# Hybrid retention/mLSTM layer on one core: weight sums begun in the first retention heads, mixing PSUM pools swapped, last two gate projections one behind the other

## The chip, the cores and the metric

One core of one Trainium2 chip runs the whole layer as one program. The metric is device time in microseconds (us) of an execution, lower is better. The kernel before takes 1399.98 us, the median of 3 runs between 1396.87 and 1403.07.

## The reference

One decoder layer for 1024 prompt positions and 8 samples of 8 positions, 1088 columns (tokens) together, all in float32:

```python
h = rmsnorm(x, pre_mix_g);  proj = (h @ w_in)          # q, k, v, gate of 4 retention and 4 mLSTM heads, 8 gate rows
ret_y = head_groupnorm(retention_chunked(rotary(q_r), rotary(k_r), v_r, S_ret)) * silu(g_r)
ml_y  = head_groupnorm(mlstm_chunked(q_m, k_m, v_m, i_pre, f_pre, C, n, m)) * sigmoid(o_m)
x = x + rmsnorm(concat([ret_y, ml_y]) @ w_out, post_mix_g)
h2 = rmsnorm(x, pre_ffn_g);  up = h2 @ w_up            # 2 x 2816 columns
conv = causal depthwise convolution of width 3 over up
x = x + rmsnorm((gelu(conv_gate) * conv_val) @ w_down, post_ffn_g)
```

The outputs are x and the new states (retention S, mLSTM C, n, m, the last rows of `up`).

## The kernel before, in words

Activations lie transposed, features on the 128 partitions and tokens along the free axis, in four blocks of 272 columns. Every float32 product is made of three fast ones: both factors are split into a rounded half and the rest (`split_w`, `gain_split`: ACT writes `hi`, DVE subtracts to `lo`), and `dense` (lines 152 to 161) runs 8 x 3 matmuls of 128x272 into one PSUM bank for one weight tile and one block.

**Mixing.** `proj` multiplies one 128-column tile of `w_in` with the four blocks; the weight comes by SyncE (SP) through a staging ring `wst` of two buffers and is split into a ring `whi`/`wlo` of two. The 32 projections go two PSUM banks (`psA`), everything else of the heads six (`psB`). `mix_head` does the four retention heads, then the four mLSTM heads; `front` transposes k and v of a pair of chunks and makes the scores, `pair_of` carries the state, `sample` does the eight samples, `finish` the group norm. Between the pairs of chunks `next(rows)` issues a piece of other work: in retention heads 1 to 3 the chain of the mLSTM gate rows (`gate_rows`, operations on 4x1088 values and two scans on DVE), in the mLSTM heads the weight sums.

**Weight sums.** The up-projection uses Strassen's seven products for 20 of its 22 feature tiles, and these need sums of quarters of `w_up`. `weight_sums` (line 688) makes them on GpSimd (POOL): 40 parts, each of two loads of 256 KB from POOL's own DMA queue, four additions of 128x256 and one store of 512 KB to the scratch tensor `sd`. It uses three buffers, the thirds of the tile `tab`. `tab` also holds the rotation tables (first two thirds) and the retention constants (the last third), so its first two thirds are free once the last retention head has rotated its k (L443) and the last third once that head is finished (L598).

**End of mixing.** The output gates of the mLSTM heads are projections 28 to 31 (`late_gate`: DVE multiplies out of PSUM, L471, ACT takes the sigmoid, L473, DVE multiplies into `yT`, L474). The last two run side by side: for each block both weights, then `mix_split` of that block (ACT `mh` L746, DVE `ml` L747), which makes the operands of `w_out`. Those operands take the memory of `h`. Then `mixctx.close()` gives back the memory of all mixing tiles and the pool `fp` takes the same place; weights 2 and 3 of `w_out` (`wtile`), the accumulators `oacc` and the rows `xr` lie there. `out_proj(0)` runs the eight tiles of `w_out` on block 0, one group of 24 matmuls each.

What sets the order: all instructions are issued in program order by the source, a scheduler at build time sets the order on each engine, and each engine then works through its own list strictly in that order. `tc.issue_after` chains one instruction behind another on the same engine; all weight sums are one chain.

## Time and profile before

| | |
|---|---|
| runs | 1399.98 us median (1396.87 to 1403.07) |
| profiled execution | 1397.98 us, its span 1396.0 us |
| mean granted TensorE clock | 0.989 of full |
| PE busy | 1346.0 us, 96% of the span |
| DVE, ACT, POOL busy | 1025.8, 587.9, 476.9 us |
| weight sums on POOL, first to last | 258.6 to 569.3 us |
| last mixing matmul ends / first `w_out` group is evacuated | 552.8 / 560.0 us |

A busy PE is at its work nearly everywhere; what a change can give back are the stretches where it waits. They are found with the list of waits and then looked at in the order of time. Times within the span are counted from its start.

### The profile page before, as it was taken

The page shows a single profiled execution, that of the slowest core. Times are in us where ns is not written, and L with a number is a line of the kernel's source. Part 1 is how long each engine was busy: PE and PEld are TensorE (multiplying, and loading weights), DVE is VectorE, ACT ScalarE, POOL GpSimd, SP SyncE. Part 2 cuts the span into 40 slices and gives each one's busy share as a digit, 9 for nine tenths or more (in the row PEclk, how much of TensorE's full clock was granted, in tenths as well). Part 3 has the DMA queues.
Part 4 walks back from the last instruction along what each step waited for, and adds up shares of the span by engine and source line. Part 5 has one row for each costly group of instructions (what it writes and reads, how often), then busy time and mean ns, then how long its engine had stood idle before and what let it go on. Part 6 is the DMA issues. An engine that isn't in the chain of part 4 may idle for free.

```text
span 1396.0 us, 26912 instructions
## 1 busy us (share of the span) xinstructions
PE 1346.0 (96%) x10545; PEld 1320.9 (95%) x10545; DVE 1025.8 (73%) x2023; ACT 587.9 (42%) x1102; POOL 476.9 (34%) x605
## 2 busy tenths in 40 slices
PE   7999899999999998699999999999999999999995
PEld 7899899999999998699999999999999999999995
DVE  7845985465475578457889987787787788996677
ACT  6423642312222334345565443443343355554563
POOL 4200000129669769200443322212222216782000
PEclk9999999999999999799999999999999999999998
DMA  6111112227876986523314444334444359533363
GB/s 238 61 46 64 48 63 62 93 81 215 206 167 228 211 178 193 202 80 97 111 60 139 162 141 139 125 122 140 147 139 138 110 166 320 181 118 97 91 215 128
DMA packets 92878, 192.80 MB, mean 138 GB/s; under 512 B 16208, under 2 KB 41040, under 8 KB 92240
## 3 DMA queue, kind: packets, MB, share of 16 engines
q1 hardware_dynamic: 80592, 149.14, 32.8%
q0 software_dynamic: 12160, 41.95, 11.7%
q8 instruction: 83, 1.36, 0.4%
q14 instruction: 43, 0.35, 0.1%
HBM read 134.58 MB, written 56.47 MB: 137 GB/s over the span
## 4 chain that ended last, share of the span: by engine, by line
PE 68%; POOL 12%; DVE 8%; DMA 6%; issue 5%; ACT 2%; DVEq 0%; SPq 0%; ACTq 0%; POOLq 0%
POOL tab L700 10%; PE up_S L972 6%; PE up_S L971 6%; PE up_S L970 6%; PE dn L1167 5%; PE dn L1169 5%; PE dn L1168 5%; PE up_A L971 4%; PE up_A L970 4%; PE up_A L972 4%; PE in L161 4%; PE in L159 4%; PE in L160 4%; DMA tab<-in_wu 2%; DMA sd<-tab 2%
## 5 line engine op out<-in xcount | busy, mean ns | idle before, releaser
L159 PE MATMUL in<-hh,wh_in 128*128 128x272 f32 x1024 | 303.0, 296 | 10.9 <-ACT hh L199 6.4
L161 PE MATMUL in<-hh,wl_in 128*128 128x272 f32 x1024 | 300.5, 294 | 1.0 <-DVE wl_in L147 0.9
L160 PE MATMUL in<-hl,wh_in 128*128 128x272 f32 x1024 | 299.4, 293 | 1.2 <-DVE hl L200 1.2
L159 PEld LDWEIGHTS in<-hh,wh_in 128*128 128x128 f32 x1024 | 194.8, 190 | 13.7 <-ACT hh L199 6.4
L160 PEld LDWEIGHTS in<-hl,wh_in 128*128 128x128 f32 x1024 | 194.8, 190 | 3.7 <-issue 2.1
L161 PEld LDWEIGHTS in<-hh,wl_in 128*128 128x128 f32 x1024 | 194.3, 190 | 2.5 <-DVE wl_in L147 1.5
L145 ACT ACTIVATE wh_up<-st_up 128x1024 fp32r<-128x1024 f32 x84 | 80.5, 959 | 165.2 <-PE up_S L971 99.5
L700 POOL TENSOR_TENSOR tab<-tab 128x256 f32<-128x256 f32 x160 | 131.9, 835 | 20.2 <-DMA tab<-in_wu 12.9
L147 DVE TENSOR_TENSOR wl_up<-st_up,wh_up 128x1024 fp32r<-128x1024 f32 x84 | 95.5, 1137 | 8.4 <-ACT wh_up L145 8.4
L944 DVE TENSOR_TENSOR Uv<-Uv,up_S 128x272 f32<-128x272 f32 (+1 forms) x200 | 66.6, 375 | 46.3 <-PE up_S L972 46.3
L1096 DVE TENSOR_TENSOR rb<-rb 128x544 fp32r<-128x544 f32 x78 | 74.0, 955 | 35.3 <-ACT rb L1095 35.2
L1000 POOL TENSOR_TENSOR act<-act 128x544 f32<-128x544 f32 x44 | 70.6, 1604 | 78.3 <-DMA bd<-act 53.3
L700 POOL DMA_DIRECT2D tab<-in_wu x80 | 56.8, 717 | 89.0 <-DVE k_r L443 32.4
L1116 POOL TENSOR_TENSOR wd<-wd 128x512 f32<-128x512 f32 x44 | 74.4, 1718 | 25.1 <-issue 11.2
L1095 ACT ACTIVATE rb<-rb 128x544 fp32r<-128x544 f32 x78 | 50.6, 651 | 75.1 <-DMA rb<-bd 69.6
L985 DVE SCALAR_TENSOR_TENSOR c<-Uv,vec,c 128x1024 f32<-128x1024 f32 (+1 forms) x88 | 70.0, 798 | 8.9 <-ACT c L983 8.9
L985 DVE SCALAR_TENSOR_TENSOR c<-Ug,vec,c 128x1024 f32<-128x1024 f32 x88 | 67.5, 806 | 1.4 <-ACT c L983 1.4
L983 ACT ACTIVATE c<-Ug,vec 128x1024 f32<-128x1024 f32 (+1 forms) x44 | 34.7, 835 | 52.6 <-DVE Ug L948 46.9
L623 POOL TENSOR_TENSOR vx_r<-vts,cst 64x1024 f32<-64x1024 f32 x3 | 5.9, 1963 | 143.1 <-ACT vts L537 143.1
L145 ACT ACTIVATE wh_in<-st_in 128x1024 fp32r<-128x1024 f32 x32 | 33.9, 1058 | 48.9 <-PE in L160 45.9
L159 PE MATMUL out<-mh,wh_out 128*128 128x272 f32 x128 | 39.7, 310 | 13.5 <-ACT wh_out L145 11.1
L147 DVE TENSOR_TENSOR wl_in<-st_in,wh_in 128x1024 fp32r<-128x1024 f32 x32 | 40.7, 1272 | 10.6 <-ACT wh_in L145 9.8
(541 smaller groups left out, 4648.6 us busy)
## 6 DMA issues: line engine op xcount, KB each, us to landing
rb<-bd SPq DMA_DIRECT2D x76, 272.0 KB, 2.8
tab<-in_wu POOLq DMA_DIRECT2D x80, 256.0 KB, 4.8
sd<-tab POOLq DMA_DIRECT2D x40, 512.0 KB, 4.2
st_up<-sd SPq DMA_DIRECT2D x40, 512.0 KB, 3.9
bd<-act SPq DMA_DIRECT2D x33, 544.0 KB, 4.6
st_in<-in_wi SPq DMA_DIRECT2D x32, 512.0 KB, 4.4
st_up<-in_wu SPq DMA_DIRECT2D x24, 512.0 KB, 3.4
wd<-in_wd SPq DMA_DIRECT2D x44, 256.0 KB, 5.0
```

The costliest lines, as they stand in the source:

```text
L145: nc.scalar.activation(hi, x, AF.Copy)
L147: eng.tensor_tensor(lo, x, hi.bitcast(F32), ALU.subtract)
L159: nc.tensor.matmul(ps, hi[:, ws], xh, start=k == 0, stop=False)
L160: nc.tensor.matmul(ps, hi[:, ws], xl, start=False, stop=False)
L161: nc.tensor.matmul(ps, lo[:, ws], xh, start=False, stop=k == KT - 1)
L700: last["sums"] = f(*args)
L970: nc.tensor.matmul(ps, wh[:, c], xh[:, k, n], start=k == 0, stop=False)
L971: nc.tensor.matmul(ps, wh[:, c], xl[:, k, n], start=False, stop=False)
L972: nc.tensor.matmul(ps, wl[:, c], xh[:, k, n], start=False, stop=k == 3)
L985: nc.vector.scalar_tensor_tensor(c, u(i), cw(i), c, ALU.mult, ALU.add)
L1096: nc.vector.tensor_tensor(lo, x, hi.bitcast(F32), ALU.subtract)
L1116: nc.gpsimd.tensor_tensor(quad(p, out), quad(p, x), quad(p, y), op)
```

## The change

1. **Weight sums earlier and with a buffer of their own.** A new tile `wq` (128x1024) takes the place of the rings `wt` and `qs` of the mLSTM heads, in the long-lived pool `mp` just behind `tab`. The first 13 parts use `wq` alone, load, add, store, one after the other with nothing fetched ahead; they are issued in the retention heads 0 to 2, from the early gates of head 0 on. Parts 13 to 17, issued in retention head 3, use the first two thirds of `tab` and `wq` with two fetched ahead; parts 18 to 39, issued in the mLSTM heads, use the three thirds of `tab` as before. The chain now begins behind the last square of `square_sum`.
2. **POOL work moved to DVE.** The three memsets of the gate rows and the multiplication `vx` of retention heads 0 to 2 go to DVE.
3. **PSUM pools swapped**: `psB` (six banks) first, then `psA` (two), so that the first banks of the pool that follows are those of `psB`.
4. **Projections 30 and 31** run one behind the other; `mix_split` follows each block of 31.

```diff
     mixctx = ExitStack()
+    psB = mixctx.enter_context(tc.tile_pool(name="psB", bufs=6, space=PSUM))
     psA = mixctx.enter_context(tc.tile_pool(name="psA", bufs=2, space=PSUM))
-    psB = mixctx.enter_context(tc.tile_pool(name="psB", bufs=6, space=PSUM))
...
+    wq = mp.tile([P, 2, 2, 2 * P], F32, name="wq")
...
-        nc.gpsimd.memset(rst, 1.0)
+        nc.vector.memset(rst, 1.0)
...
                 for i in range(NH):
                     proj((12 + i, early_gate(i)))
+                    next(wsums)
...
-                wt = m2.tile([P, 2, P], F32, tag="wt", name=f"wt_{nmc}")
+                wt, qs = (wq[:, turns["wq"] % 2, i].rearrange("p (i n) -> p i n", i=2) for i in range(2))
...
-            e = nc.vector if hid > 2 else nc.gpsimd
-            e.tensor_tensor(vx, vt[:TS, 0, :W].unsqueeze(1).broadcast_to([TS, NB, W]),
+            nc.vector.tensor_tensor(vx, vt[:TS, 0, :W].unsqueeze(1).broadcast_to([TS, NB, W]),
...
             next(rows, None)
+            if hid > 2 or i % 2 == 0:
+                next(wsums, None)
...
+        own = wq.rearrange("p a b n -> p (a b) n")
+        free = [tab[:, i * D:(i + 1) * D].rearrange("p (b n) -> p b n", b=4) for i in range(3)]
...
+        def stretch(i0, i1, tiles, ahead):
+
+            for i in range(i0, min(i0 + ahead, i1)):
+                fetch(i, tiles[(i - i0) % len(tiles)])
+            for i in range(i0, i1):
                 j, c = parts[i]
...
+                g = tiles[(i - i0) % len(tiles)]
+                if ahead == 0:
+                    fetch(i, g)
+                a11, a22, a12, a21 = (g[:, n, :] for n in range(4))
+                for o_, x, y, op in ((a21, a11, a21, ALU.subtract), (a22, a22, a21, ALU.subtract),
+                                     (a11, a22, a11, ALU.add), (a12, a12, a22, ALU.subtract)):
+                    queued(nc.gpsimd.tensor_tensor, o_, x, y, op)
+                queued(nc.gpsimd.dma_start, sd[j][:, :, cols(c)], g)
+                if 0 < ahead and i + ahead < i1:
+                    fetch(i + ahead, tiles[(i + ahead - i0) % len(tiles)])
                 yield

+        yield from stretch(0, 13, [own], 0)
+        yield from stretch(13, 18, [free[0], free[1], own], 2)
+        yield from stretch(18, len(parts), free, 2)
...
-    proj((30, late_gate(6)), (31, late_gate(7)), done=mix_split)
+    proj((30, late_gate(6)))
+    proj((31, late_gate(7)), done=mix_split)
```

How the built programs differ at three places. On POOL, behind the last square (`sq1`), the kernel before has the `vx` of three heads and the memsets, and then the weight sums in `tab`:

```order
L206 TENSOR_TENSOR sq1_130<-x3_93 128x272
L623 TENSOR_TENSOR vx_r0_1405<-vts2_268,cst_81 64x8x128
L357 MEMSET yT2_803 4x1088
L359 MEMSET yT2_803 4x8
L360 MEMSET yT2_803 4x8
L623 TENSOR_TENSOR vx_r1_2017<-vts1_267,cst_81 64x8x128
L623 TENSOR_TENSOR vx_r2_2638<-vts0_266,cst_81 64x8x128
L700 DMA tab_82<-in_wu 128x2x256 x4
L700 TENSOR_TENSOR tab_82<-tab_82 128x256 x4
L700 DMA sd_276<-tab_82 512x1x256
```

Now the sums follow the last square at once, thirteen times load, add, store in `wq`:

```order
L206 TENSOR_TENSOR sq1_131<-x3_94 128x272
L705 DMA wq_83<-in_wu 128x2x256 x2
L705 TENSOR_TENSOR wq_83<-wq_83 128x256 x4
L705 DMA sd_277<-wq_83 512x1x256
L705 DMA wq_83<-in_wu 128x2x256 x2
```

Nothing on POOL waits for the heads any more until the first part that uses `tab`.

On DVE in retention head 1, among the gate rows (`yT2`, `yT3`, `fg` are their rows; `k_r1` is the rotated k, `in5_0` block 0 of its projection), before, two scans (L362, L368) and eight short ones (L372) stand ahead of the addition that completes block 0 of k (L445):

```order
L354 SCALAR_TENSOR_TENSOR fg_1543<-fg_1543,yT2_803 4x1088
L443 TENSOR_TENSOR k_r1_1640<-in5_0_1777,tab_82 128x272
L444 TENSOR_TENSOR sw_kr10_1802<-sw_kr10_1802,tab_82 128x272
L445 TENSOR_TENSOR q_r1_1639<-q_r1_1639,sw_qr13_1765 128x272
L362 SCALAR_TENSOR_TENSOR yT2_803<-yT2_803,fg_1543 4x1088
L368 SCALAR_TENSOR_TENSOR yT3_804<-fg_1543,yT3_804 4x1024
L372 SCALAR_TENSOR_TENSOR yT3_804<-fg_1543,small_275,yT3_804 4x8 x8
L445 TENSOR_TENSOR k_r1_1640<-k_r1_1640,sw_kr10_1802 128x272
```

Now only the large memset stands between, and the scans come behind it, the one that needs the memsets (L363) later still:

```order
L444 TENSOR_TENSOR k_r1_1690<-in5_0_1827,tab_82 128x272
L445 TENSOR_TENSOR sw_kr10_1852<-sw_kr10_1852,tab_82 128x272
L355 SCALAR_TENSOR_TENSOR fg_1593<-fg_1593,yT2_804 4x1088
L358 MEMSET yT2_804 4x1088
L616 COPY qx_271<-q_r1_1689 128x8x8
L446 TENSOR_TENSOR k_r1_1690<-k_r1_1690,sw_kr10_1852 128x272
L444 TENSOR_TENSOR k_r1_1690<-in5_1_1858,tab_82 128x272
L445 TENSOR_TENSOR sw_kr11_1883<-sw_kr11_1883,tab_82 128x272
L369 SCALAR_TENSOR_TENSOR yT3_805<-fg_1593,yT3_805 4x1024
L373 SCALAR_TENSOR_TENSOR yT3_805<-fg_1593,small_276,yT3_805 4x8 x8
```

The two scans have moved from ahead of block 0 of k to behind it.

On DVE at the end of mixing (`z_7` and `in31_3` are the last gate and its block 3; `ml_10`, `ml_11` the operands of blocks 2 and 3, `wl_out1` the second weight of `w_out`), before:

```order
L471 TENSOR_TENSOR z_7_6540<-in31_3_6778,rb_83 128x272
L747 TENSOR_TENSOR ml_10_6742<-yT0_801,mh_10_6741 128x2x272
L747 TENSOR_TENSOR ml_10_6742<-yT1_802,mh_10_6741 128x2x272
L147 TENSOR_TENSOR wl_out1_6845<-st_out1_6842,wh_out1_6844 128x1024
L747 TENSOR_TENSOR ml_11_6744<-yT2_803,mh_11_6743 128x2x272
L747 TENSOR_TENSOR ml_11_6744<-yT3_804,mh_11_6743 128x2x272
```

Now, with `ml_01` the second half of blocks 0 and 1:

```order
L472 TENSOR_TENSOR z_7_6619<-in31_3_6742,rb_84 128x272
L758 TENSOR_TENSOR ml_10_6731<-yT0_802,mh_10_6730 128x2x272
L758 TENSOR_TENSOR ml_10_6731<-yT1_803,mh_10_6730 128x2x272
L475 TENSOR_TENSOR yT3_805<-yT3_805,z_7_6619 128x272
L758 TENSOR_TENSOR ml_01_6657<-yT3_805,mh_01_6656 128x2x272
L147 TENSOR_TENSOR wl_out1_6806<-st_out1_6803,wh_out1_6805 128x1024
```

Between the last evacuation and `wl_out1` stand two more operations of the gates and splits.

## Rows read from the trace of the kernel before

**Rows 1.** The page, part 1: busy time, share and count of each engine.

```profile
PE 1346.0 (96%) x10545; PEld 1320.9 (95%) x10545; DVE 1025.8 (73%) x2023; ACT 587.9 (42%) x1102; POOL 476.9 (34%) x605
```

**Rows 2.** The list of waits of PE over the whole span: what waited, for what, us in total, times, longest.

```profile
PE out L159 <- ACT wh_out L145: 11.1, 2, 10.7
...
PE x_r L525 <- DVE k_r L445: 2.9, 1, 2.9
...
PE in L159 <- DVE A_m L598: 1.5, 1, 1.5
...
PE in L159 <- DVE z L471: 0.9, 1, 0.9
...
PE in L159 <- DVE q_r L443: 0.8, 2, 0.7
```

**Rows 3.** PE in order of time at the end of mixing: start, duration, operation, and in brackets the idle time before it and what ended it.

```profile
552.51 0.29 PE L161 MATMUL in<-hh,wl_in 128*128 128x272 f32 x1
...
555.22 0.36 PE L159 MATMUL out<-mh,wh_out 128*128 128x272 f32 x1 [2.42 <-ACT mh L746]
...
573.74 0.56 PE L159 MATMUL out<-mh,wh_out 128*128 128x272 f32 x1 [10.72 <-ACT wh_out L145]
```

**Rows 4.** PE by stretches: length, busy time (matmuls), granted clock, DMA share, GB/s.

```profile
556.00:559.40 3.40, 3.40 (x17) 0.51 0.47 176
...
573.70:580.00 6.30, 5.86 (x24) 0.50 0.97 360
```

**Rows 5.** ACT in order of time in the first block of the output projection: `oacc` and `mo` evacuate a group, `wh_out` and `woh` split a weight.

```profile
572.30 0.40 ACT L807 ACTIVATE oacc<-out 128x272 f32<-128x272 f32 x1 [8.59 <-DMA sd<-tab]
...
573.82 1.06 ACT L145 ACTIVATE wh_out<-st_out 128x1024 fp32r<-128x1024 f32 x1
...
582.60 1.06 ACT L145 ACTIVATE woh<-st_out 128x1024 fp32r<-128x1024 f32 x1
...
589.62 1.05 ACT L145 ACTIVATE woh<-st_out 128x1024 fp32r<-128x1024 f32 x1
...
593.48 0.49 ACT L805 ACTIVATE mo<-out,vec 128x272 f32<-128x272 f32 x1 [2.14 <-PE out L161]
...
596.52 0.49 ACT L805 ACTIVATE mo<-out,vec 128x272 f32<-128x272 f32 x1 [2.26 <-PE out L161]
```

**Rows 6.** POOL in order of time: the last square, the first load whose buffer is the last third of `tab`, the last store.

```profile
48.34 0.77 POOL L206 TENSOR_TENSOR sq<-x 128x272 f32<-128x272 f32 x1 [0.38 <-DVE sums_sb L210]
...
306.43 0.72 POOL L700 DMA_DIRECT2D tab<-in_wu  x1 [12.46 <-DVE A_r L598]
...
568.55 0.74 POOL L700 DMA_DIRECT2D sd<-tab  x1 [0.30 <-POOL tab L700]
```

**Rows 7.** The additions of the weight sums by their line (ns minimum/median/maximum, first and last start), and from the page's DMA issues the loads and stores of the sums and the loads of `w_out` (KB each, median us to landing).

```profile
L700 POOL TENSOR_TENSOR tab<-tab x160: 714/738/1797, 267.7 to 567.5; 128x256 f32<-128x256 f32 x160
...
tab<-in_wu POOLq DMA_DIRECT2D x80, 256.0 KB, 4.8
sd<-tab POOLq DMA_DIRECT2D x40, 512.0 KB, 4.2
...
st_out<-in_wo SPq DMA_DIRECT2D x8, 512.0 KB, 4.7
```

**Rows 8.** DVE in order of time in retention head 1, among the gate rows.

```profile
158.76 2.41 DVE L362 TENSOR_TENSOR_SCAN yT<-yT,fg 4x1088 f32<-4x1088 f32 x1
161.09 2.25 DVE L368 TENSOR_TENSOR_SCAN yT<-fg,yT 4x1024 f32<-4x1024 f32 x1
163.27 1.16 DVE L372 TENSOR_TENSOR_SCAN yT<-fg,small,yT 4x8 f32<-4x8 f32 x8
164.36 0.42 DVE L445 TENSOR_TENSOR k_r<-k_r,sw_kr 128x272 f32<-128x272 f32 x1
...
173.69 0.28 DVE L666 COPY S_r<-u_r 128x128 f32<-128x128 f32 x1
```

**Rows 9.** DVE beside an idle and a busy POOL. The split of `w_in` weights from 60 to 250 us and from 306 to 526 us (busy us, mean ns | idle before); two operations of 128x544 by line (ns minimum/median/maximum); and all engines by stretches (length; busy us of PE, PEld, DVE, ACT, POOL; clock, DMA share, GB/s).

```profile
L147 DVE TENSOR_TENSOR wl_in<-st_in,wh_in 128x1024 fp32r<-128x1024 f32 x11 | 13.4, 1220 | 2.3 <-ACT wh_in L145 2.3
...
L147 DVE TENSOR_TENSOR wl_in<-st_in,wh_in 128x1024 fp32r<-128x1024 f32 x12 | 15.7, 1306 | 2.9 <-ACT wh_in L145 2.1
...
L747 DVE TENSOR_TENSOR ml<-yT,mh x16: 712/1246/1265, 538.8 to 563.4; 128x544 fp32r<-128x544 f32 x16
...
L835 DVE TENSOR_TENSOR xr<-xr x8: 710/718/726, 608.4 to 698.6; 128x544 f32<-128x544 f32 x8
...
40.00:60.00 20.00, 18.51 (x144) 17.98 (x143) 18.73 (x41) 10.28 (x23) 6.52 (x8) 1.00 0.19 64
...
125.00:150.00 25.00, 25.00 (x190) 23.05 (x190) 19.83 (x68) 14.23 (x31) 0.00 (x0) 1.00 0.30 92
150.00:175.00 25.00, 21.11 (x167) 20.40 (x166) 24.94 (x52) 12.76 (x24) 1.15 (x3) 1.00 0.08 24
...
306.00:450.00 144.00, 144.00 (x1134) 137.33 (x1133) 83.11 (x252) 38.09 (x110) 114.86 (x151) 1.00 0.75 198
525.00:550.00 25.00, 22.57 (x178) 22.16 (x177) 20.39 (x35) 9.77 (x19) 23.10 (x29) 1.00 0.60 188
```

**Rows 10.** The multiplication `vx` on DVE as the mLSTM heads have it, and a one-input DVE operation on 4x1088 values, by line.

```profile
L623 DVE TENSOR_TENSOR vx_m<-vts,cst x4: 1226/1254/1408, 331.2 to 491.8; 64x1032 f32<-64x1032 f32 x4
...
L342 DVE TENSOR_SCALAR yT<-yT x1: 708/708/708, 145.7 to 145.7; 4x1088 f32<-4x1088 f32 x1
```

More of the change, by code (lines that the diff above doesn't have):

```diff
@@ L205, in square_sum @@
             if k:
-                nc.gpsimd.tensor_tensor(o_, x[:, k, :], x[:, k, :], ALU.mult)
+                last["sums"] = nc.gpsimd.tensor_tensor(o_, x[:, k, :], x[:, k, :], ALU.mult)
             else:
@@ L356, in gate_rows @@
         rst = e
-        nc.gpsimd.memset(rst, 1.0)
+        nc.vector.memset(rst, 1.0)
         rp, rs_ = chunked(rst)
-        nc.gpsimd.memset(rp[:, :, 0:1], 0.0)
-        nc.gpsimd.memset(rs_[:, :, 0:1], 0.0)
+        nc.vector.memset(rp[:, :, 0:1], 0.0)
+        nc.vector.memset(rs_[:, :, 0:1], 0.0)
         bb = w1
@@ L477, in hybrid_layer_kernel @@
     EARLY = (0, 1, 2, 3)
+    turns = {"wq": 0}
     early = []
@@ L545, in front @@
                     nc.tensor.matmul(flat2(0), sel[:, 0, hd, :], uihl[:, cs_], start=True, stop=False)
-                wt = m2.tile([P, 2, P], F32, tag="wt", name=f"wt_{nmc}")
+                wt, qs = (wq[:, turns["wq"] % 2, i].rearrange("p (i n) -> p i n", i=2) for i in range(2))
+                turns["wq"] += 1
                 for i, c in enumerate(cs):
@@ L556, in front @@
                                           flat2(1).rearrange("p (s l) -> p s l", s=NB)[:, :, LS - 1])
-                qs = m2.tile([P, 2, P], F32, tag="qs", name=f"qs_{nmc}")
                 qv = q[:, c0 * CH:c0 * CH + L * n].rearrange("p (i n) -> p i n", i=L)
@@ L621, in sample @@
             vx = m2.tile([TS, NB, 129], F32, tag="vx", bufs=1, name=f"vx_{nm}")[:, :, :W]
-            e = nc.vector if hid > 2 else nc.gpsimd
-            e.tensor_tensor(vx, vt[:TS, 0, :W].unsqueeze(1).broadcast_to([TS, NB, W]),
-                            cst[:TS, C_BLK:C_BLK + NB].unsqueeze(2).broadcast_to([TS, NB, W]), ALU.mult)
+            nc.vector.tensor_tensor(vx, vt[:TS, 0, :W].unsqueeze(1).broadcast_to([TS, NB, W]),
+                                    cst[:TS, C_BLK:C_BLK + NB].unsqueeze(2).broadcast_to([TS, NB, W]), ALU.mult)
             if ml:
-                e.tensor_tensor(sb, sb, dec[:, 8:16].unsqueeze(2).broadcast_to([P, NB, W]), ALU.mult)
+                nc.vector.tensor_tensor(sb, sb, dec[:, 8:16].unsqueeze(2).broadcast_to([P, NB, W]), ALU.mult)
             step = 3 if ml else 4
@@ L694, in weight_sums @@
         cols = lambda c: slice(c * 256, c * 256 + 256)
-        held = []
+        own = wq.rearrange("p a b n -> p (a b) n")
+        free = [tab[:, i * D:(i + 1) * D].rearrange("p (b n) -> p b n", b=4) for i in range(3)]
         def queued(f, *args):
-            with tc.issue_after(last["sums"].ins) if "sums" in last else nullcontext():
+            with tc.issue_after(last["sums"].ins):
                 last["sums"] = f(*args)
-        def fetch(i):
-            if i < len(parts):
-                j, c = parts[i]
-                g = tab[:, i % 3 * D:(i % 3 + 1) * D].rearrange("p (b n) -> p b n", b=4)
-                for q in range(2):
-                    queued(nc.gpsimd.dma_start, g[:, q::2, :], a["wu"][j, q].rearrange("p (b n) -> p b n", b=2)[:, :, cols(c)])
-                held.append(g)
@@ L710, in weight_sums, with fetch @@
-        fetch(0)
-        fetch(1)
-        for i, (j, c) in enumerate(parts):
-            g = held.pop(0)
-            a11, a22, a12, a21 = (g[:, i, :] for i in range(4))
-            for o_, x, y, op in ((a21, a11, a21, ALU.subtract), (a22, a22, a21, ALU.subtract),
-                                 (a11, a22, a11, ALU.add), (a12, a12, a22, ALU.subtract)):
-                queued(nc.gpsimd.tensor_tensor, o_, x, y, op)
-            queued(nc.gpsimd.dma_start, sd[j][:, :, cols(c)], g)
-            fetch(i + 2)
-            if c:
+        def fetch(i, g):
+            j, c = parts[i]
+            for q in range(2):
+                queued(nc.gpsimd.dma_start, g[:, q::2, :], a["wu"][j, q].rearrange("p (b n) -> p b n", b=2)[:, :, cols(c)])
@@ L721, in weight_sums @@
                 yield
+        yield from stretch(0, 13, [own], 0)
+        yield from stretch(13, 18, [free[0], free[1], own], 2)
+        yield from stretch(18, len(parts), free, 2)
+    wsums = weight_sums()
     rows = iter(())
@@ L730, in hybrid_layer_kernel @@
         pass
-    rows = weight_sums()
     for hd in range(NH):
         mix_head(hd, True)
-    for _ in rows:
+    for _ in wsums:
         pass
```

## The prediction

> **What bounds the kernel now.** I read the page's busy times first: PE is busy 96% of the span [rows 1], so no other engine is the bound, and a change can only give back time in which PE waits or runs at a lower clock. The list of waits says where: of its long entries one stands far ahead, 11.1 us in which the output projection waited for the split weight `wh_out`; then come 2.9 us for a rotated k, 1.5 for `A_m`, 0.9 for a gate evacuation and 0.8 for the rotation of q [rows 2]. In the order of time the end of mixing shows it. The last mixing matmul ends at 552.8, the first group of the output projection begins 2.42 us late, and 10.72 us are lost before the third [rows 3]. ACT tells why: it stood 8.59 us in front of the evacuation `oacc` until the last store of the weight sums had landed, and the splits of weights 2 and 3 stand behind that [rows 5]. `oacc` and these weights lie where `tab` lay, and POOL issued its last store only at 568.55 [rows 6]. The clock adds to it: granted 0.51 from 556 to 559.4 and 0.50 from 573.7 to 580 [rows 4], that is the lower of its two levels (1.2 of 2.4 GHz), each time after PE had waited. The eighth group's evacuation follows its matmuls at 596.5 [rows 5], so from the last mixing matmul to the end of block 0 are 43.6 us. A group without waits takes 3.04 us (596.52 less 593.48 [rows 5]), eight take 24.3: 19.3 us are lost here.
>
> **Part 1, the weight sums.** Do they now end in time? One part in `wq` alone: the second load is issued 0.7 after the first and lands 4.8 later, four additions of 0.74, 4.2 until the store has landed [rows 7], 0.3 in front of it [rows 6]: about 13 us. Thirteen parts from the last square at 49 [rows 6] take until about 219. Two thirds of `tab` come free with head 3's k; the first addition in them started at 267.7 [rows 7]. The last third comes free at 306.4 [rows 6], and parts 13 to 18 fit between. Before, the 39 parts from then until ACT went on at 572.3 took 265.9 us, 6.8 each, with every stall in them. Now 21 are left: 306 + 21 x 6.8 = 449. So `tab` is free some 100 us before it is wanted, and the stall of 10.72 us goes for certain; it would come back only if a part took over 11.7 us ((552.8 - 306.4) / 21).
>
> What is late next? Call E the end of the last mixing matmul. Weight 0 of `w_out` takes the ring place of projection 30, free 12 us before E, so group 0 can begin at E; its operands (`mh_00`, `ml_00` to `ml_01`) need the end of block 1 of projection 31, 6 us before E, and about 3.5 us of DVE at 0.71 a piece without POOL beside it [rows 9]. Weight 1 takes the place of projection 31, free only at E. Its ACT split waits behind five `mh` pieces and a sigmoid, its DVE split behind `ml_10` and `ml_01`: ready near E + 4.3, while group 0 ends at E + 3.0. Wait 1.1. Weight 3 uses the staging buffer of weight 1: load from E + 4.3, landing 4.7 later [rows 7], ACT split 1.06: E + 10. On PE the first matmuls of group 3 stand ahead of most of group 2, so group 2 waits for it too: from E + 7.3 to E + 10, 2.7 us. Weights 4 to 7 then have a cycle of load and two splits near 7.3 us for two buffers, against 6.1 of PE: I count 1.4 us of waits together. A fall of the clock as between 556 and 559.4 costs 3.4 - 17 x 0.127 = 1.3 us [rows 4], and it came after 2.42 and 0.89 us of waits; after a single wait of 2.9 in the stretch from 150 to 175 it did not come (clock 1.00 [rows 9]). I take half, 0.7. Sum: 24.3 + 1.1 + 2.7 + 1.4 + 0.7 = 30.2 instead of 43.6, **13.4 us gained**. The bounds: 19.3 if nothing waits; if weights 2 to 7 come at the pace at which they came before, a pair in 7.0 to 8.8 us (573.82, 582.60, 589.62 [rows 5]), say 3.9 each, block 0 ends at E + 10 + 23.4 + 1.3 = 34.7 and 8.9 are gained.
>
> **Part 2, POOL work on DVE, and POOL's new company.** The order on DVE changes with it. The memset of 4x1088 costs DVE 0.7 (as the one-input operation of that size [rows 10]). With it the scheduler has put both scans behind block 0 of k. Before, that k waited for 2.41 + 2.25 + 1.16 us of scans [rows 8] and PE for it 2.9 [rows 2]. Now k is ready about 4.5 us earlier, and PE does not wait there. But it comes then to the state copy `S_r`, before at 173.69 [rows 8], which stands behind the same operations: I put it at 172.2, so 1.5 us of the 2.9 remain gained. The wait of 0.7 us for q [rows 2] in the same chain goes too, since the large gate operation now stands behind that q. `vx` costs DVE 1.25 [rows 10] three times, in places where PE has matmuls; in head 1 the POOL `vx` had held DVE up as long. Gain 2.2.
>
> Against this stands POOL's arithmetic, which now runs while heads 0 and 1 need DVE: 3 us of every 13, 23%. The nearest rows: with POOL busy 114.86 of 144 us the split `wl_in` took 1306 ns instead of 1220, 7% more; with POOL busy 23.1 of 25 us `ml` took 1075 ns as a mean (16.5 us for 16), a like operation beside an idle POOL 718, half as much again [rows 9]. Scaled to 23% that is 2 to 13%. DVE is full from 150 to 175 (24.94 of 25 [rows 9]) and PE waits for it there; with the stretches from 40 to 60 and 125 to 150 (18.73 and 19.83 [rows 9]) 63 us of DVE are exposed: 1.3 to 8.2 us. Most of these operations read two SBUF tensors, but PE has slack in half of these stretches; I take 2.5, nearer the lower row, which holds more operations. Net of part 2: **0.3 lost**, between 3.6 gained (all waits of the heads gone, no contention) and 8.2 lost.
>
> The Trainium skill, "SBUF — State Buffer", section "SBUF: two separate sides", says that DVE and GpSimd share one port pair under an exclusive lock, held for the whole instruction, and that the loser blocks fully, also where the DVE operation has two SBUF inputs. The `ml` rows [rows 9] look like it, the `wl_in` rows far less; taken to the letter in every one of the additions it is the second rival below.
>
> **Parts 3 and 4.** Side by side, projections 30 and 31 held both banks of `psA`; PE waited 0.9 us for an evacuation [rows 2]. One behind the other this goes: 0.9. `A_m` cost 1.5 [rows 2]; PE now comes there 1.2 us earlier, but DVE has some six operations in front of `A_m` that POOL no longer slows by up to 0.36 each, as it did `ml` [rows 9], 2 us: 0.7 gained, between 1.2 lost and 1.5 gained. The swapped pools give groups 0 and 1 banks that are long free; the wait of 2.42 us is counted in part 1.
>
> **Sum.** Against the profiled execution, 1397.98 us: -13.4 + 0.3 - 0.9 - 0.7 = -14.7, so 1383.3. The median of the runs is 2.0 above the profiled one: **1385 us** for the median. What this measurement can tell from no change is about 0.5%, 7 us.
>
> **Rivals.** *Weights bound block 0* (12%). The stall goes, but block 0 runs at the pace of its weights, gain 8.9 as above: -8.9 + 0.3 - 1.6 = -10.2, 1390. For it: the SP queue has 1.7 MB of other loads (two of 544 KB, one of 396, one of 256) in front of weight 4. Against: these are issued at E + 6 now and have landed when weight 4 is needed.
>
> *POOL holds DVE up in the retention heads* (12%, 5% of it slower). One mechanism at one place: 52 additions of 0.74 us [rows 7], 38.5 us, beside the DVE chains of heads 0 to 2, on which PE hangs. If each addition held DVE up in full and PE with it, 38.5 would stand in the sum in place of 2.5, which is then 21.3 slower: 1421. It decides from the point where 17.2 of the 38.5 us reach PE, 45%; between 10 and 24 us it is no measurable change, about 1400. Against: in the mLSTM heads POOL was busy 80% of the time and PE did not wait at all (144.00 of 144 [rows 9]). For it: DVE is not full there, and in head 0 it is.
>
> *The stall stays* (4%). If the parts with one buffer take so long that the rest still ends after E, only the 1.6 us of parts 3 and 4 remain, some 1399. Part 1 shows how far away that is.
>
> **How the numbers follow.** The forecast has 72%, its own range 1380 to 1391: from 19.3 at the boundary to some 9. The first rival lies in 1387 to 1394. Faster by over 0.5% (under 1393) are the forecast and most of the first rival: 81%. Within 0.5%: the mild form of the second, the third and a little of the others, 13%. Slower: 6%. The range for 8 in 10 goes from 1378 to 1396: the lower end is the boundary without any wait and the retention waits half gone, the upper one contention near its upper bound (8.2 instead of 2.5) together with weights at the old pace.
>
> **What would show it.** Right: the last store on POOL before 470 us; no wait of ACT or PE for a store `sd`; between E and the end of block 0 about 30 us with two waits of PE, 1 and near 3 us, for `wl_out` and `wh_out`; PE's wait for k in head 1 under 1 us. Wrong: PE idle that rises by over 5 us before 260; a part in `wq` of over 16 us; a new wait before E for an operand `mh` or `ml`, since `mix_split` now begins later; or block 0 over 35 us.

## The result and the profile after

The changed kernel takes 1385.44 us, the median of 6 runs between 1384.45 and 1387.14; the kernel before, on the same chip, 1398.86 (6 runs, 1393.23 to 1403.07). The ratio is 0.9908, 95% interval 0.9885 to 0.9930: 13.4 us less. In a later set of runs it was 0.9873 (0.9858 to 0.9888). The profiled execution took 1387.14 us (span 1385.4), the longest of its six; this matters below.

The list of waits of PE after, to be read against [rows 2]: what waited, for what, us in total, times, longest. The 11.1 us for `wh_out` are 0.4, and the waits for `mh`, for `A_m` and for `z` ahead of the last projections are gone. New or longer are 1.8 for q, 1.3 for `rcol` (a small product in retention head 0), 1.2 for `S_r` (0.3 before), 1.1 for `wol` (0.7 before), 1.1 for `z`, and 0.9 each for `woh` and for an output matmul whose releaser the view does not name ("issue").

```profile
PE in L159 <- DVE q_r L444: 1.8, 1, 1.8
...
PE o_r L664 <- DVE S_r L668: 1.2, 1, 1.2
PE out L161 <- DVE wol L147: 1.1, 2, 0.7
...
PE x_r L528 <- DVE k_r L446: 0.7, 1, 0.7
PE out L159 <- ACT wh_out L145: 0.4, 1, 0.4
```

PE in order of time at the end of mixing (start, duration, operation, idle time before it), as [rows 3]. The last row is the sum of squares over the third block of the output projection, a fixed place that serves below as the end of this stretch.

```profile
554.06 0.29 PE L161 MATMUL in<-hh,wl_in 128*128 128x272 f32 x1
555.43 0.36 PE L159 MATMUL out<-mh,wh_out 128*128 128x272 f32 x1 [1.08 <-DVE z L472]
...
562.64 0.36 PE L159 MATMUL out<-mh,wh_out 128*128 128x272 f32 x1 [0.89 <-issue]
...
563.54 0.40 PE L159 MATMUL out<-mh,wh_out 128*128 128x272 f32 x1 [0.41 <-ACT wh_out L145]
...
570.60 0.39 PE L159 MATMUL out<-mh,woh 128*128 128x272 f32 x1 [0.88 <-ACT woh L145]
...
571.86 0.39 PE L161 MATMUL out<-mh,wol 128*128 128x272 f32 x1 [0.75 <-DVE wol L147]
...
578.51 0.39 PE L161 MATMUL out<-mh,wol 128*128 128x272 f32 x1 [0.37 <-DVE wol L147]
...
638.04 0.73 PE L186 MATMUL ssqb_po<-oacc,ones 128*128 128x272 f32 x2 [0.44 <-DVE oacc L821]
```

The same sum in the kernel before:

```profile
649.95 0.73 PE L186 MATMUL ssqb_po<-oacc,ones 128*128 128x272 f32 x2 [0.44 <-DVE oacc L809]
```

So from the end E of the last mixing matmul, 554.35 (554.06 + 0.29), to that sum are 83.69 us; before they were 649.95 - 552.80 = 97.15. The boundary gave 13.46. But E itself is 1.55 later than before (1.17 if both are counted from PE's first matmul). And 1.3 us are lost again behind that sum: from 670.1 to 673.5 PE had half the clock, behind a wait of 2.52 us for the sum over the fourth block; in the kernel before the same wait, 2.53 us, was not followed by a lower clock.

POOL after: the first part, the last store from `wq`, the first load into `tab`, the last store of all ([rows 6] has its place before, 568.55).

```profile
49.52 1.62 POOL L705 DMA_DIRECT2D wq<-in_wu  x2
53.88 4.36 POOL L705 TENSOR_TENSOR wq<-wq 128x256 f32<-128x256 f32 x4 [2.74 <-DMA wq<-in_wu]
...
221.63 0.75 POOL L705 DMA_DIRECT2D sd<-wq  x1 [0.30 <-POOL wq L705]
260.26 0.71 POOL L705 DMA_DIRECT2D tab<-in_wu  x1 [37.88 <-DVE k_r L444]
...
446.82 0.74 POOL L705 DMA_DIRECT2D sd<-tab  x1 [0.30 <-POOL tab L705]
```

ACT in the first block, as [rows 5]: the splits of weights 2 and 3 and of 4, and the eighth group. No wait for `sd` is left.

```profile
561.49 2.00 ACT L145 ACTIVATE wh_out<-st_out 128x1024 fp32r<-128x1024 f32 x2
...
569.48 1.06 ACT L145 ACTIVATE woh<-st_out 128x1024 fp32r<-128x1024 f32 x1 [1.74 <-DMA st_out<-in_wo]
...
585.10 0.49 ACT L817 ACTIVATE mo<-out,vec 128x272 f32<-128x272 f32 x1 [2.74 <-PE out L161]
```

By stretches, as [rows 4] (length; busy time of PE, PEld, DVE, ACT, POOL; clock, DMA share, GB/s): PE keeps the full clock over the whole boundary, where it had fallen to half twice.

```profile
553.00:584.00 31.00, 26.63 (x200) 25.30 (x200) 17.84 (x26) 18.78 (x33) 0.46 (x4) 1.00 0.53 176
```

### The profile page after: what moved, and what is told of

It is laid out like the page before. It is cut to its first block, busy times and chain, and to the rows that moved or that the text cites. A ratio compares the mean times of both kernels' runs of the same rounds, so it can differ in the third digit from the quotient of the medians.

```text
span 1385.4 us, 26923 instructions
## 1 busy us (share of the span) xinstructions
PE 1346.3 (97%) x10545; PEld 1319.4 (95%) x10545; DVE 1019.1 (74%) x2029; ACT 588.4 (42%) x1102; POOL 477.8 (34%) x599
## 3 DMA queue, kind: packets, MB, share of 16 engines
q8 instruction: 83, 1.36, 0.4%
## 4 chain that ended last, share of the span: by engine, by line
PE 86%; DVE 8%; ACT 2%; issue 2%; DMA 2%; DVEq 0%; SPq 0%; ACTq 0%
PE in L161 9%; PE in L160 8%; PE in L159 8%; PE up_S L984 6%; PE up_S L983 6%; PE up_S L982 6%; PE dn L1179 4%; PE dn L1181 4%; PE dn L1180 4%; PE up_A L983 4%; PE up_A L982 4%; PE up_A L984 4%; PE out L161 2%; PE out L160 2%; PE out L159 2%
## 5 line engine op out<-in xcount | busy, mean ns | idle before, releaser
L705 POOL TENSOR_TENSOR tab<-tab 128x256 f32<-128x256 f32 x104 | 82.4, 802 | 11.0 <-DMA tab<-in_wu 6.6
L705 POOL TENSOR_TENSOR wq<-wq 128x256 f32<-128x256 f32 x56 | 55.1, 994 | 48.9 <-DMA wq<-in_wu 46.6
L705 POOL DMA_DIRECT2D tab<-in_wu x52 | 36.8, 713 | 61.3 <-DVE k_r L444 41.9
```

What stands on the lines that cost most here:

```text
L705: last["sums"] = f(*args)
```

## The experiments

Two places of every profile are compared in this table: E counted from the start of PE's first matmul (that start varies by 0.8 us between executions), and the stretch from E to the sum over the third block. The chips differ: on them the kernel before had medians from 1398.86 to 1403.99, so the ratio to the kernel before on the same chip stands beside each time. The changed kernel itself was timed in two sets (rows after and e11); e1 to e4 and e12 ran on one chip, e5 to e8 on a second, e9 to e11 on a third. Where medians of different chips are compared below, part of the difference can be the chip's.

| run | E | E to sum | median us (runs) | ratio (95%) |
|---|---|---|---|---|
| before | 546.43 | 97.15 | 1398.86 (6) | |
| after | 547.60 | 83.69 | 1385.44 (6) | 0.9908 (0.9885-0.9930) |
| e1 part 2 alone | 546.13 | 97.45 | 1399.31 (12) | 0.9970 (0.9952-0.9988) |
| e2 parts 3, 4 alone | 545.29 | 103.29 | 1402.26 (12) | 0.9988 (0.9972-1.0004) |
| e3 parts 1, 2 | 546.99 | 83.70 | 1385.49 (5) | 0.9866 (0.9844-0.9887) |
| e4 13 parts without additions | 544.74 | 83.89 | 1384.84 (4) | 0.9862 (0.9840-0.9884) |
| e5 sums from head 2 | 544.91 | 84.81 | 1385.54 (6) | 0.9907 (0.9891-0.9923) |
| e6 part 2 undone | 557.80 | 84.80 | 1398.33 (12) | 1.0000 (0.9986-1.0015) |
| e7 weights 2, 3 elsewhere | 545.33 | 86.97 | 1389.45 (6) | 0.9930 (0.9911-0.9946) |
| e8 = e5 + e7 | 545.92 | 86.15 | 1387.17 (6) | 0.9922 (0.9905-0.9940) |
| e9 weights 4, 5 elsewhere | 545.31 | 80.95 | 1382.29 (4) | 0.9853 (0.9839-0.9866) |
| e10 vx on POOL | 556.54 | 84.89 | 1398.20 (5) | 0.9965 (0.9951-0.9978) |
| e11 after again | 544.70 | 84.42 | 1384.46 (4) | 0.9873 (0.9858-0.9888) |
| e12 = e5 + e9 | 545.18 | 80.99 | 1380.86 (5) | 0.9841 (0.9827-0.9854) |

**Which part makes the gain (e1 to e3).** e1 is the kernel before with part 2 alone:

```diff
-        nc.gpsimd.memset(rst, 1.0)
+        nc.vector.memset(rst, 1.0)
...
-            e = nc.vector if hid > 2 else nc.gpsimd
+            e = nc.vector
```

> The kernel before, with only the memsets and the vx products of the retention heads moved from POOL to DVE; the weight sums still begin in the mLSTM heads. If the new order on DVE in head 1 is a gain by itself and the additions of POOL are what made the last mixing matmul late in the changed kernel (theory): PE's wait for the rotated k falls from 2.9 to under 1.5 us, its wait for q goes, the last mixing matmul ends near 551 instead of 552.8, the stall for the weight sums stays near 11 us, and the run takes about 2 us less, 1396 to 1397. If DVE's extra work itself made it late (rival): the last mixing matmul ends at 554 or later and the run is 1 to 3 us slower than the kernel before.

The wait for k fell to 1.68 us and the stall stayed at 10.79, but E came only 0.3 us earlier, not 2: the wait for q stayed, and 2.2 us of waits stood ahead of E for gate evacuations. The median is 4.7 us below that of the kernel before, which spread there from 1397.5 to 1410.3; the profile shows no gain at the boundary, so where those 4.7 are from stays open. DVE's added work did not make the mixing late.

e2 is the kernel before with parts 3 and 4 alone:

```diff
+    psB = mixctx.enter_context(tc.tile_pool(name="psB", bufs=6, space=PSUM))
     psA = mixctx.enter_context(tc.tile_pool(name="psA", bufs=2, space=PSUM))
-    psB = mixctx.enter_context(tc.tile_pool(name="psB", bufs=6, space=PSUM))
...
-    proj((30, late_gate(6)), (31, late_gate(7)), done=mix_split)
+    proj((30, late_gate(6)))
+    proj((31, late_gate(7)), done=mix_split)
```

> The kernel before, with only the swapped PSUM pools and projections 30 and 31 one behind the other. Theory (the early weight sums make the gain): ACT still waits for the last store of the sums, near 568.5, PE still stalls by 10 us or more, since the 1.6 us won ahead of it are waited away in front of the same store; 1397 to 1399, 0 to 1.6 us gained. Rival (the banks and the projections make most of the gain): the stall shrinks to under 3 us and the run takes 1386 to 1389.

The waits of 1.5 and 0.9 us ahead of E went and E came 1.1 earlier, but then ACT stood 12.98 us in front of the store and PE 14.95. In order of time, PE and ACT of e2:

```profile
555.18 0.57 PE L159 MATMUL out<-mh,wh_out 128*128 128x272 f32 x1 [3.86 <-ACT mh L746]
...
579.02 0.57 PE L159 MATMUL out<-mh,wh_out 128*128 128x272 f32 x1 [14.95 <-ACT wh_out L145]
```

```profile
577.58 0.40 ACT L808 ACTIVATE oacc<-out 128x272 f32<-128x272 f32 x1 [12.98 <-DMA sd<-tab]
```

What was won ahead of the store was waited away in front of it. The last store itself was issued at 573.84, 5.3 us later than in the kernel before, so the stretch from E on is longer by more than the 1.1 us that were won (6.1); what made it later this run does not show. The time is no different from the kernel before. e3 is the changed kernel with both these edits undone (pools in the old order too):

```diff
...
-    proj((30, late_gate(6)))
-    proj((31, late_gate(7)), done=mix_split)
+    proj((30, late_gate(6)), (31, late_gate(7)), done=mix_split)
```

> The changed kernel with the PSUM pools in their old order and projections 30 and 31 side by side again. Theory: the stall for the sums stays gone, the waits of 0.9 us for an evacuation and of up to 2.4 us for the first mh come back, 1386 to 1389, that is 1 to 3.5 us above the changed kernel. Rival (banks and projections make most of the gain): 1394 or more, with PE standing over 6 us between the last mixing matmul and the end of the first block.

Its stretch from E on is 83.70 us, that of the changed kernel 83.69, and its median, on another chip, is the same to 0.1 us: the waits of 0.9 and 1.5 us do not come back, nor does one for `mh`. With parts 1 and 2 these waits are gone without parts 3 and 4, which then win nothing that this run shows.

**What POOL's company costs in the retention heads (e4, e5, e11).** e4 leaves the four additions out for parts 0 to 12:

```diff
-                                     (a11, a22, a11, ALU.add), (a12, a12, a22, ALU.subtract)):
+                                     (a11, a22, a11, ALU.add), (a12, a12, a22, ALU.subtract)) if i >= 13 else ():
```

> The changed kernel without the four additions of each of the first 13 parts of the weight sums: these parts are only loaded and stored again, so 13 of the 34 column halves of the combined up weights hold their raw quadrants. Theory (POOL's additions hold DVE up in the retention heads): the last mixing matmul ends near 551 instead of 554.4, PE's waits for rotated q and k and for S_r in heads 0 and 1 fall by 2 to 4 us together, the run takes 1381 to 1383. Rival (the transfers of these parts, or DVE's own added work): the last mixing matmul stays within 0.7 us of 554.4 and the run within 1 us of the changed kernel, 1384.5 to 1386.

E came at 551.30, 3.05 us before that of the changed kernel, as the theory had it, but the median (on another chip) is only 0.6 lower; in the profile PE later waited once 1.36 us for a split of the down projection. e5 keeps the additions and moves them away from heads 0 and 1:

```diff
+            if hd == 2:
+                nc.vector.tensor_copy(wq[:, 0, 0, 0:1], q[:, 0:1])
...
-                    next(wsums)
...
-            if hid > 2 or i % 2 == 0:
+            if hid > 1:
...
-        yield from stretch(0, 13, [own], 0)
-        yield from stretch(13, 18, [free[0], free[1], own], 2)
-        yield from stretch(18, len(parts), free, 2)
+        yield from stretch(0, 5, [own], 0)
+        yield from stretch(5, 10, [free[0], free[1], own], 2)
+        yield from stretch(10, len(parts), free, 2)
```

> The changed kernel, but the sums begin only with retention head 2, behind its rotated q (a copy of one column into their buffer holds the first load back), with 5 parts in the small buffer instead of 13. Theory (POOL's additions hold DVE up in heads 0 and 1): the last mixing matmul ends 2.5 to 3.5 us earlier than in the changed kernel, 551 to 552, the last store of the sums moves from 447 to about 500 us, still ahead of the output projection, and the run takes 1382 to 1384. Rival (the additions cost as much wherever they stand, since DVE has work in every head): last mixing matmul at 553.5 to 554.5, run 1385 to 1386. Rival (the sums need the early start): the stall for a store comes back, 1388 or more.

E again 2.9 us earlier, the last store at 498.29, no stall, and yet a median equal to that of the changed kernel. In the first block PE had half the clock from 570.0 to 573.4, which takes back part of it (84.81 us from E to the sum). So I ran the changed kernel again:

> The changed kernel once more, as it is, for the spread of the place where the last mixing matmul ends. If what POOL's additions cost in the retention heads depends on where they happen to fall (theory): it ends between 545 and 548 us counted from the start of the first matmul, PE's single waits in heads 0 and 1 differ from those of the first profile, and the time is again 1385 to 1386. If the cost is the same in every run (rival): 547.5 to 547.7 with the same waits of 1.8, 0.7 and 1.2 us.

In this execution E is 544.70 from the first matmul, 2.9 us earlier than in the first one: no q is waited for, while the waits for k and `S_r` are the same to the hundredth. PE in order of time in head 1 of e11:

```profile
167.37 0.30 PE L528 MATMUL x_r<-cst,k_r 128*128 128x128 f32 x1 [0.74 <-DVE k_r L446]
...
173.56 0.49 PE L664 MATMUL o_r<-S_r,q_r 128*128 128x128 f32 x2 [1.20 <-DVE S_r L668]
```

The five profiles with these same heads (after, e3, e7, e9, e11) have E at 547.60, 546.99, 545.33, 545.31 and 544.70, a mean of 545.99; with the first 13 parts silent or later (e4, e5, e8, e12) it is 544.74 to 545.92, a mean of 545.19. With the early sums E comes 0.8 us later on average, with a spread of 2.9 us from profile to profile, and the first profile showed the upper end. e4 and e5 also have another order on DVE (the scans ahead of the rotated k, a wait of 1.68 for it), so these 0.8 us are not contention alone.

One wait does come with the additions in every profile. PE stood 1.31 to 1.50 us in front of `rcol`, near 60 us, in all seven whose first parts are added in head 0 (after, e3, e6, e7, e9, e10, e11) and in none of the other seven. The four additions of the first part fall there (53.88 to 58.24 in the changed kernel). PE in the first profile, then DVE in it and in e4, which has no additions there:

```profile
60.35 0.81 PE L274 MATMUL rcol<-cst,rb 128*128 128x1 f32 x6 [1.32 <-DVE rb L192]
```

```profile
55.90 1.75 DVE L147 TENSOR_TENSOR wl_in<-st_in,wh_in 128x1024 fp32r<-128x1024 f32 x1
57.58 1.32 DVE L268 TENSOR_TENSOR tab<-tab,rb 128x272 f32<-128x272 f32 x2
```

```profile
55.44 1.22 DVE L147 TENSOR_TENSOR wl_in<-st_in,wh_in 128x1024 fp32r<-128x1024 f32 x1
56.58 0.79 DVE L268 TENSOR_TENSOR tab<-tab,rb 128x272 f32<-128x272 f32 x2
```

With 0.20 us on the operation before them (L192, 0.63 instead of 0.43) DVE lost 1.26 us there, and PE waited about as long for the next L192. In head 1 the order gives some of it back: the waits are 0.74 and 1.20 us in e11 and 0.69 and 1.68 in e5, so 1.33 less 0.43 is 0.9, close to the 0.8 of the means.

The 1.84 us for q that only the first profile has came another way. That q stood behind ACT, and ACT in front of the load `xsel`, which could start only when the store `out_ss` had left its buffer. First profile, then e11:

```profile
132.07 0.60 SPq L639 DMA_DIRECT2D out_ss<-sb_r  x1
137.26 0.33 SPq L293 DMA_DIRECT2D xsel<-in_cx  x1
```

```profile
140.99 1.06 ACT L299 ACTIVATE sel<-xsel 100x1024 fp32r<-100x1024 f32 x1 [4.24 <-DMA xsel<-in_cx]
```

```profile
131.25 0.60 SPq L639 DMA_DIRECT2D out_ss<-sb_r  x1
134.88 0.33 SPq L293 DMA_DIRECT2D xsel<-in_cx  x1
```

```profile
138.60 1.06 ACT L299 ACTIVATE sel<-xsel 100x1024 fp32r<-100x1024 f32 x1 [2.21 <-DMA xsel<-in_cx]
```

From the store to the load are 5.19 us in the first and 3.63 in the second. POOL issued a store of its own 0.18 us behind `out_ss` in the first and 0.99 behind it in e11; whether the two transfers hindered each other is not shown. e4, which has these transfers without additions, waits 0.73 us for a q near that place. And e3 has half the clock for 6.8 us from 60.0, the other four of these five for 3.4; by estimate that is 1.7 of the 2.3 us that its E is later than in e11. So the spread of 2.9 us is not the additions' alone.

**Part 2 as what makes part 1 possible (e6, e10).** e6 puts memsets and `vx` of the retention heads back on POOL (the edit of `vx` stands at e10):

```diff
-        nc.vector.memset(rst, 1.0)
+        nc.gpsimd.memset(rst, 1.0)
...
```

> The changed kernel with the memsets and the vx products of the retention heads back on POOL, where they now stand in its queue among the parts of the sums. Theory (with early sums POOL is no place for work that DVE and PE wait for, since its queue stands still while a part is loaded and stored): the memset waits behind a part's store and load, the scans and vx come late, PE waits 3 to 10 us more in heads 0 to 2, the last mixing matmul ends at 557 to 564 and the run takes 1388 to 1395. Rival (it makes no difference on which of the two they stand): last mixing matmul within 1 us of 554.4, 1384.5 to 1386.5. Rival (DVE's added work is what made the mixing late): 551 to 553, 1382 to 1384.

All of the gain is gone. e10 puts back `vx` alone:

```diff
+            e = nc.vector if hid > 2 else nc.gpsimd
-            nc.vector.tensor_tensor(vx, vt[:TS, 0, :W].unsqueeze(1).broadcast_to([TS, NB, W]),
+            e.tensor_tensor(vx, vt[:TS, 0, :W].unsqueeze(1).broadcast_to([TS, NB, W]),
```

> The changed kernel with only the three vx products of the retention heads back on POOL (the memsets stay on DVE). Theory (a product that PE waits for stands in POOL's queue behind a load and a store of the sums, and the wait of PE brings the clock down): PE waits over 3 us for vx in head 0, runs at a lower clock for some us after it, the last mixing matmul ends 5 to 9 us later than in the changed kernel, 1391 to 1396. Rival (it is the memset, and the scans behind it, that cost in the run with both): less than 3 us lost, 1385 to 1388.

E comes 11.84 us later than in e11 (556.54 from the first matmul against 544.70), in e6 13.10 later: nearly all of it is `vx`. The two medians are alike, but from two chips; e10 is still 4.4 us below the kernel before on its own. POOL of e10 in order of time:

```profile
122.67 1.41 POOL L706 DMA_DIRECT2D wq<-in_wu  x2 [2.89 <-DMA sd<-wq]
129.06 2.99 POOL L706 TENSOR_TENSOR wq<-wq 128x256 f32<-128x256 f32 x4 [4.98 <-DMA wq<-in_wu]
132.02 1.89 POOL L626 TENSOR_TENSOR vx_r<-vts,cst 64x1024 f32<-64x1024 f32 x1
```

PE of e10, and its stretches:

```profile
133.96 3.77 PE L634 MATMUL us_r<-vx_r,kz_r 64*128 64x512 f32 x4 [4.73 <-POOL vx_r L626]
```

```profile
134.00:140.00 6.00, 6.00 (x14) 3.46 (x15) 2.73 (x10) 0.12 (x1) 2.00 (x3) 0.50 0.40 129
...
175.00:200.00 25.00, 22.64 (x162) 20.63 (x161) 24.94 (x55) 11.84 (x22) 14.76 (x16) 0.93 0.31 106
```

`vx` stands in POOL's queue behind four additions which wait 4.98 us for a load to land; PE waits 4.73 us for it, then runs at half its clock (0.50 from 134 to 140), and the clock falls again between 175 and 200, behind a wait of 2.36 us for k. The 4.73 us, half of the 10.2 us at half the clock (5.1, an estimate) and waits for q and k of 4.6 us in place of 1.9 add up to 12.5, about what E lost.

**What bounds the first block now (e7, e8, e9, e12).** e7 gives weights 2 and 3 buffers of their own:

```diff
...
-            wo.append(load_w(a["wo"][m], f"out{m}", *wtile()))
+            st = utile(f"st_out{m}", 0)[:, :D] if m > 1 else None
+            wo.append(split_w(stage_w(a["wo"][m], f"out{m}", st), f"out{m}", *wtile()))
```

> The changed kernel with weights 2 and 3 of the output projection loaded into two buffers of the up projection's columns, which are idle then, so that no load of the first four waits for a staging buffer. Theory (after the stall it is the staging of weights 2 to 7 that PE waits for in block 0): PE's waits of 0.4 to 0.9 us for splits of weights in block 0 go, 2 to 2.5 us together; from the last mixing matmul to the end of the third block 81.5 us instead of 83.7, run 1383 to 1383.5. Rival (block 0 is bound by something else, the transfers or ACT's and DVE's queues): the waits move to weights 4 to 7 and the run stays at 1385 to 1386.

It is slower, and in another way than either theory. ACT of e7, then PE and the clock:

```profile
559.35 2.00 ACT L145 ACTIVATE woh<-st_out 128x1024 fp32r<-128x1024 f32 x2
...
562.47 1.06 ACT L145 ACTIVATE wh_out<-st_out 128x1024 fp32r<-128x1024 f32 x1 [0.46 <-DMA st_out<-in_wo]
...
563.92 1.06 ACT L145 ACTIVATE wh_out<-st_out 128x1024 fp32r<-128x1024 f32 x1 [0.39 <-DMA st_out<-in_wo]
```

```profile
563.63 0.36 PE L159 MATMUL out<-mh,wh_out 128*128 128x272 f32 x1 [4.01 <-issue]
...
565.03 0.60 PE L159 MATMUL out<-mh,wh_out 128*128 128x272 f32 x1 [0.90 <-ACT wh_out L145]
```

```profile
564.00:571.00 7.00, 6.10 (x28) 5.97 (x28) 2.02 (x2) 2.04 (x2) 0.53 (x4) 0.51 0.82 325
```

The scheduler loaded weights 4 and 5 (`woh`) into the staging buffers ahead of 2 and 3 (`wh_out`), whose new buffers come free only at the end of mixing; PE waited 4.01 and 0.90 us for what it needs first and then had half the clock. The edit had not built what it was meant to try. e8 has the same and the late sums:

> The two edits of the runs before it together: sums from retention head 2 on, weights 2 and 3 of the output projection in buffers of their own. Theory: both gains add up, 1380 to 1382. Rival (what is won before the output projection is waited away behind it): 1383 or more.

It loses in the same way: 86.15 us from E to the sum, 1387.17 in all.

e9 does it the other way round, weights 4 and 5 in those buffers:

```diff
...
-            wo.append(split_to(stage_w(a["wo"][m], f"out{m}"), hi, lo))
+            st = utile(f"st_out{m}", 0)[:, :D] if m < 6 else None
+            wo.append(split_to(stage_w(a["wo"][m], f"out{m}", st), hi, lo))
```

> The changed kernel with weights 4 and 5 of the output projection loaded into two idle buffers of the up projection, so that their loads stand on SP right behind that of weight 3 and weights 6 and 7 have the two staging buffers for themselves. Theory (after the stall, PE's waits in block 0 are for the staging of weights 4 to 7): the three waits of 0.4 to 0.9 us for splits of weights 4 to 7 go, the two of 0.9 and 0.4 for weight 3 stay; 2 us less from the last mixing matmul to the end of the third block (81.7 instead of 83.7), run 1383 to 1384. Rival (as with weights 2 and 3, the buffers are free too late or the transfers crowd each other): weight 3 lands later, PE waits 1 us or more longer for it and the clock falls; 1386 to 1390.

PE of e9: three waits are left of the six, and the stretch is 80.95 us.

```profile
552.69 0.36 PE L159 MATMUL out<-mh,wh_out 128*128 128x272 f32 x1 [1.08 <-DVE z L472]
...
559.89 0.37 PE L159 MATMUL out<-mh,wh_out 128*128 128x272 f32 x1 [0.88 <-issue]
...
560.79 0.39 PE L159 MATMUL out<-mh,wh_out 128*128 128x272 f32 x1 [0.41 <-ACT wh_out L145]
```

On the same chip as e11 it takes 2.2 us less (1382.29 against 1384.46, ranges 1380.80 to 1383.02 and 1383.61 to 1385.72). e12 adds the late sums:

> The version with weights 4 and 5 in idle buffers, and with it the sums begun only in retention head 2. Theory (the additions cost PE in heads 0 and 1 from nothing to 3 us, by where they fall, so that a later start takes away only a spread and no more than 1 us of the median, while PE's waits in block 0 stay as short): last mixing matmul 544.7 to 546 us after the first, run 1381 to 1382.5. Rival (the later start gives its own gain of some 2.5 us on top, as the profile of that run alone suggested): 1379 to 1380.5. Rival (it collides with the weights in block 0, as with weights 2 and 3 in those buffers): 1384 or more.

1380.86 (1379.95 to 1381.72), the best version here; the further 1.4 us against e9 come from another chip and lie between what the two theories gave.

## Why the prediction was right, step by step

**The stall (part 1).** Right: a part in `wq` 13.6 us as a mean ((221.63 + 4.2 - 49.52) / 13, with the 4.2 of [rows 7] for the last store to land), forecast 13; thirteen parts done by 226, forecast 219; the last store issued at 446.82, where the forecast had `tab` free at 449; no wait of ACT or PE for `sd`. e2 and e3 show that parts 3 and 4 are not needed for the gain; that part 1 needs part 2 stands below.

**What is late next.** From E to the sum 13.46 us were gained in the first profile and 12.7 in e11 (97.15 - 84.42); forecast 13.4. In the prediction's own measure block 0 ended at E + 30.75 (585.10 - 554.35) instead of E + 30.2, and 13.0 us were gained (43.7 by its rows, not 43.6, less 30.75). The terms came out otherwise. Wait 1.1 for `wl_out1`: PE did wait 1.08, but for the evacuation `z` of the last gate, ahead of group 0; `wl_out1` was ready at E + 4.3, as forecast, and nothing waited for it. Wait 2.7 for weight 3: 0.41, since its split was done at E + 9.1 instead of E + 10, and 0.89 ahead of that for the split of weight 2, which ended at 562.55 and which its sum has nowhere. Weights 4 to 7: 2.00 (0.88 + 0.75 + 0.37) instead of 1.4, and e9 took exactly these waits away. The clock: nothing instead of 0.7 (and half of a fall is 0.6 by [rows 4]: 3.4 less 17 x 0.127 is 1.24, not 1.3). Together 4.4 instead of 5.9. The rest of block 0 then took 26.4 us where eight groups without waits were put at 24.3. In e9, with the waits for weights 4 to 7 gone, that rest is 25.1 (27.48 - 2.37), so about half of the 2.1 went with them; why is open. That 13.4 fits so well is partly luck: the waits were put too high and the work too low.

**Part 2, the order.** Forecast 2.2: k wait 1.5 less, q gone. In e11 the waits in head 1 are 0.74 + 1.20 = 1.94 instead of 2.91 + 0.69 + 0.29 = 3.89, of which [rows 2] shows the first two: 1.95 gained. The memset took 0.96 instead of 0.7.

**Part 2, the contention.** Forecast 2.5 lost in every run. The step that failed is that I scaled a mean slowdown of DVE, where PE pays only when a burst of additions falls on a chain that it waits for: here once, 1.3 to 1.5 us in front of `rcol`, in every profile. The first profile, with 1.84 us for q on top, has 3.2, not far from 2.5, by luck: that wait hung on the landing of a transfer. Elsewhere DVE lost time too, and no wait of PE that these profiles show goes with it. DVE in head 1 of the first profile, with POOL beside it, and POOL:

```profile
176.91 1.82 DVE L381 TENSOR_TENSOR yT<-yT,yT 4x1088 f32<-4x1088 f32 x1
```

```profile
170.15 7.45 POOL L705 TENSOR_TENSOR wq<-wq 128x256 f32<-128x256 f32 x4 [2.72 <-DMA wq<-in_wu]
...
302.60 3.04 POOL L705 TENSOR_TENSOR tab<-tab 128x256 f32<-128x256 f32 x4 [0.21 <-DMA tab<-in_wu]
```

This DVE operation took 1.27 us in e4, without the additions: 0.55 less, and less than one addition of 0.74 (in e11 it took 1.81, too). POOL lost far more, 7.45 instead of 3.04 us for four additions. The Trainium skill, "SBUF — State Buffer", section "SBUF: two separate sides", has the one that starts first hold the shared port pair and the other wait: these rows agree in kind, and it is POOL that waits most, beside an unbroken run of DVE work. My rival, in which each addition held up DVE and with it PE, had 38.5 us; it fell.

**Part 2, what I did not price.** I costed `vx` and the memsets against the kernel before and found nearly nothing. Against part 1 they are worth all of it: without them on DVE the changed kernel takes as long as the one before (e6), and with `vx` alone on POOL E comes 11.8 us later (e10). The prediction names POOL's queue nowhere as a cost that the edit avoids.

**Parts 3 and 4.** Forecast 1.6 gained, measured none (e3). Both waits are gone in e3 without them. That `A_m` is no longer held up by POOL fits: the first DVE operation of `A_m` took 0.68 us in the kernel before and 0.69 in e1, beside additions, and 0.15 and 0.16 in the changed kernel and e3. That belongs to part 1. But in e2, where POOL still adds at that time, it took 0.16 and the wait was gone too, so the cause is not shown to the end. The evacuation wait of 0.9, put down to the two projections side by side, goes with the early sums just as well. Counted from the first matmul, E was forecast 1.3 us earlier than before; it came 1.17 later in the first profile and 1.73 earlier in e11.

**The sum.** Own time 1383.3 forecast, 1387.14 in the first profile and 1383.61 in e11; median 1385 forecast, 1385.44 and 1384.46 measured. The three rivals did not come: no weight bound the block as in the first, the second is above, the stall did not stay.

## What to carry to other kernels

Background work on an engine that also issues its loads and stores belongs early, but then nothing that another engine waits for may stand in that engine's queue: here one product per head, 1.9 us long in head 0 and behind a load, cost 13.7 us (e10 against e11, on one chip). A buffer that is handed over at a stage boundary is released by its last store, so what is won ahead of the boundary is worth nothing until that store is early. And since E moved by 2.9 us between profiles of the same heads, read a difference of that size between two profiles only after the same kernel has been profiled twice.

## What was not expected

The spread of runs went with the stall: before, single runs lay between 1393.2 and 1410.3 us over all chips, the changed kernel's between 1383.6 and 1387.1; the spread is wide again in e6 (1396.4 to 1403.8), where PE hangs on POOL's queue in another place. That the stall is the cause is not shown: without it e7 and e8 spread over 4.3 and 5.3 us. And waits of 0.89 and 0.41 us close together left the clock at 1.00 (after, e9), while 4.01 and 0.90 in e7 and 4.73 in e10 were followed by half the clock for over 5 us, some 3 us more at each place (an estimate: half of 6 or 7 us). But like waits were not always followed alike. The 2.9 us for k in head 1 were followed by half the clock in e2 (165.1 to 168.5) and not in the kernel before; 1.08 and 0.74 us in the first block were followed by it in e5, 1.28 and 0.74 in e11 were not. So these runs give no size of wait from which the clock falls.
